# Order of the first three chunks, the planner's charge for a convolution tap, and a sum over channel tiles made by DMA

## The chip, the cores and the metric

The kernel runs on one core of a Trainium2 chip. Its time is what the device takes for one execution, in microseconds; lower is better. The core has TensorE (PE, matmuls), VectorE (DVE, elementwise work with two inputs), ScalarE (ACT, one-input functions), GpSimd (POOL, which here mostly issues DMAs that add to their target) and SyncE (SP, which issues the plain DMAs). Every engine works through its own instructions in order and waits on semaphores for the others.

## What is computed

One layer of a decoder trunk on x of 1024 positions by 1024 channels, float32:

```python
h = rms_norm(x, g_mix)
z = h @ w_in + b_in
va, ga, xb, gb, sa, sb = split(z)            # 1024, 1024, 1536, 1536, 1024, 1024
u = va * sigmoid(ga)
u = causal_depthwise_conv(u, conv_a_w, conv_a_b)       # 31 taps
y_a = silu(layer_norm(u, ln_g, ln_b)) @ w_a_out
v = rg_lru(causal_depthwise_conv(xb, conv_b_w, conv_b_b), ...)   # 4 taps, 16 heads, a scan
y_b = (v * gelu(gb)) @ w_b_out
x = x + (sigmoid(sa) * y_a + sigmoid(sb) * y_b) @ w_o
f = square(relu(rms_norm(x, g_mlp) @ w_1))
out = rms_norm(x + f @ w_2, g_final)
```

The layer norm needs, at each position, the mean over the 1024 channels of the convolved u.

## The kernel before

**Numbers.** Matmuls run on float32 values that are split in a high part h (the rounded value) and a low part l (the rest); a product takes three matmuls, h with h, h with l and l with h ("hh", "hl", "lh": the weight's part stands first in first_z, so "lh" is the weight's low part and "hl" the input's). The high part is an ACT copy. The low part is a DVE subtraction, or, in split_dma (L63), an ACT copy with its sign turned and a DMA from POOL's queue that adds the value to it in SBUF. Channels lie on the 128 partitions, positions along the free dimension, in two halves hf 0 and 1 of 512.

**The first three chunks** (L117 to L398) are the products of h with three blocks of 128 columns of w_in (block 16 of the xb part, 0 of va, 8 of ga). x comes transposed as xc in eight tiles (two halves, four pairs of channel blocks c) and plain as x in eight tiles for the sums of squares. For half 0 the norm's factor isn't known yet: x_plain and x_plain_low make the parts of x times g_mix, and the products are scaled afterwards by first_scale (L403). For half 1 x_square (L182, ACT), x_root (L195, a Newton root on DVE that leaves four diagonal tiles rd) and x_spread (L208, eight PE matmuls that spread rd over partitions as rb) make the factor first, and x_scaled (L215, DVE then ACT) and x_low (L230) the parts. All vectors of weights lie in one tile vec of 448 columns, of which columns 0 to 7 are g_mix. decay (L265) is a generator of 51 tiny DVE instructions on the recurrence's constants; decay_on(n) issues the next n. idle_mm issues matmuls of ones on nothing, ahead of the first real one. The order of ACT, DVE and PE in this block is written out by hand.

**The chunks after** (s from 3, loop at L797): each slot makes 48 matmuls for a chunk of w_in (chunk_mm, L709), those of a head of the recurrence's gates (head_mm, head_gate), and hands the chunk before to xb_out or u_out. Slot 3 does half 1 first, then scales half 0 of the first three chunks (first_scale) and makes half 0's scaled parts (first_parts, L411: xc scaled eight times, the low part three behind), then does half 0. Later come the z stage (loop at L1013: gates by a Strassen product, weights' parts zo by split_dma four steps ahead), the b branch (L1599 on: eight output tiles j, b_mm), and the branch a, w_o and the MLP.

**The convolution** of tile j is the generator conv(j) (L594): two ACT instructions that start its two accumulators, then 48 DVE steps, mostly taps of a scalar_tensor_tensor over 512 columns (L629), a store of the result to DRAM (yd[j], SP) and a last step that adds it to ysum (L641, L643). Its steps have no place of their own.

**The planner** places them. clk holds a planned time for PE, ACT and DVE; at() adds a cost. later() notes DVE work with a ready time, vector_work(end) issues it in order of ready time, and fill(until) (L433) puts taps into the DVE time that is left over:

```python
    def fill(until):
        while clk["V"] + 0.67 <= until:
...
        def step(cost=0.67):
            at("V", cost)
```

When 4 steps of a convolution are left, the ACT start of the next is issued. In the loops the limit is the planned end of PE's work in the slot. What is left after the z stage is issued in tile j = 0 of the b branch, and all that remains in j = 1 (vector_work(math.inf)).

**The mean.** n_load (L1101) reads the eight yd tiles back in 16 DMAs on SP, emitted in tile j = 0; n_mean (L1112) makes the mean by two products of ysum with a matrix of 1/1024, ahead of tile 2's matmuls; n_center, n_var, n_root and n_scale follow in tiles 2 to 5.

The tile framework puts in the waits: an instruction waits for what it reads, and a new tile waits until its slot was released.

Of the kernel before, what the change touches and what calls it, by code (L numbers as in the profile page):

```python
# [9 lines left out]
F32 = mybir.dt.float32  # L10
# [5 lines left out]
P = 128  # L16
# [14 lines left out]
def trunk_kernel(ctx: ExitStack, tc: tile.TileContext, x, xt_in, xt_eo, vecs, w_in, w_a_out, w_b_out,  # L31
# [92 lines left out]


    vec = cp.tile([P, 448], F32, name="vec")
    nc.gpsimd.dma_start(vec, vecs)
    gmix_c = vec[:, 0:8]
    bin_c = vec[:, 8:64]
# [33 lines left out]
    load_w0(1)  # L163
    load_w0(2)
    for t in range(4, 8):
        load_x(t)
# [164 lines left out]
    with tc.manual_schedule(engines={mybir.EngineType.Activation, mybir.EngineType.DVE,  # L331
# [10 lines left out]

        idle_mm(15)
        rb["tile"] = PS("rb", "ps2")
# [10 lines left out]
        for k in range(8):  # L355
            first_z(1, 0, k, "hh")
            first_z(1, 0, k, "hl")
        decay_on(6)
        first_w(2, "h")
        first_w(2, "l")  # L360
        decay_on(20)
        for t in range(4, 8):
# [6 lines left out]
        x_root(1)  # L369
        decay_on(10)  # L370
        for k in range(8):
            first_z(2, 0, k, "lh")
            if k == 4:
                x_spread(1)

        for c in range(9):
            if c < 8:
                x_scaled(1, c)
            else:
                x_root(0)  # L380
                x_spread(0)
            if 4 <= c < 8:
                x_square(c - 4, nc.scalar)
            if c:
                for which in ("hh", "lh"):
                    first_z(0, 1, c - 1, which)
                x_low(1, c - 1)
                first_z(0, 1, c - 1, "hl")
                for i in range(1, N0):
                    first_z(i, 1, c - 1, "hh")  # L390
                    first_z(i, 1, c - 1, "hl")
        for i in range(1, N0):
            for k in range(8):
                first_z(i, 1, k, "lh")
        decay()
        nc.vector.tensor_scalar(cab2, cab_c, 2.0, None, ALU.mult)
        pairs = caw[:, 8:].rearrange("p (i o j) -> p i o j", o=2, j=8)
        nc.vector.tensor_tensor(csum, pairs[:, :, 0, :], pairs[:, :, 1, :], ALU.add)  # L398


    xu = dp.tile([2, 4, P, S], F32, name="xu")

    def first_scale():  # L403

        rs = rb["d"][:, HALVES[1]]
        nc.scalar.activation(rs, rb[0], AF.Copy)
        for i in range(N0):
            o = z0[i][:, HALVES[0]]
            nc.vector.tensor_tensor(o, o, rs, ALU.mult)

    def first_parts():  # L411
        for c in range(11):
            if c < 8:
                x_scaled(0, c)
            if c > 2:
                x_low(0, c - 3)

# [6 lines left out]
    clk = {"P": 0.0, "A": 0.0, "V": 0.0}  # L424
    MM = 0.227

    def at(e, cost, ready=0.0):
# [5 lines left out]
    def fill(until):  # L433
        while clk["V"] + 0.67 <= until:
            if taps["now"] is None:
# [154 lines left out]


    NE = WA // 2 + 1

    def conv(j):  # L594
# [20 lines left out]

        def step(cost=0.67):
            at("V", cost)
            return True
# [19 lines left out]
        yield step()  # L638
        if j == 0:
            ysum.append(T("ysum"))  # L640
            nc.vector.tensor_copy(ysum[0], acc)  # L641
        else:
            nc.vector.tensor_tensor(ysum[0], ysum[0], acc, add)  # L643
        yield step(1.22)

# [62 lines left out]

    def chunk_mm(s, n0, n1, halves=(0, 1)):  # L709

        wh, wl = wst[s]
        if s not in zps:
            zps[s] = PS(f"z{s}")
        pairs = [x for k in range(8) for x in ((wh, k, 0), (wh, k, 1))] + [(wl, k, 0) for k in range(8)]
        for n in range(n0, n1):
            w, k, part = pairs[n]
            for hf in halves:
                nc.tensor.matmul(zps[s][:, HALVES[hf]], w[:, k, :], xw[k][part][hf],  # L718
                                 start=n == 0, stop=n == 23)
        at("P", len(halves) * (n1 - n0) * MM)  # L720

# [74 lines left out]
    with tc.manual_schedule(engines=ENGINES):  # L796
        for s in range(3, NC1):  # L797
            w_load(s + 2)
            taps["hold"] = s > NC1 - 4
            begun = clk["P"]  # L800
            clk["A"], clk["V"] = max(clk["A"], begun + 0.5), max(clk["V"], begun - 2)

            if s == 3:

                chunk_mm(s, 0, 24, (1,))
                first_scale()
                xb_out(0, zps[0])
                first_parts()
                chunk_mm(s, 0, 24, (0,))
            else:  # L810
# [158 lines left out]
    with tc.manual_schedule(engines=ENGINES):  # L969
# [43 lines left out]
        for n in range(len(zseq) + 2):  # L1013
            for f, *a in ZL.get(n, ()):
                f(*a)
            if n >= L:
                for f, *a in ZX.get(n, ()):
                    f(*a)
            taps["hold"] = n < 2
            clk["A"], clk["V"] = max(clk["A"], clk["P"] + 0.5), max(clk["V"], clk["P"] - 2)  # L1020
            z_get(n - 1, z_post)
# [53 lines left out]
    def b_mm(j):  # L1075
# [5 lines left out]
        else:  # L1081

            todo = [x for w, wl, h, l in ops for x in ((w, h), (w, l), (wl, h))]
        for n, (a, b) in enumerate(todo):
            for hf in range(2):
                nc.tensor.matmul(ps[hf], a, b[:, HALVES[hf]], start=n == 0, stop=n == len(todo) - 1)  # L1086
# [511 lines left out]
    with tc.manual_schedule(engines=ENGINES):  # L1598
        for j in range(8):  # L1599
            clk["A"], clk["V"] = max(clk["A"], clk["P"] + 0.5), max(clk["V"], clk["P"] - 2)  # L1600
            if j == 0:
                b_load(1)
                b_gate(0)
                n_load()
            if j == 2:
                n_mean()
            if j == 4:
# [10 lines left out]
            vector_work(clk["V"])  # L1618
            if j < 2:
                vector_work(math.inf if j else clk["P"] - 0.3)  # L1620
            elif j < 4:
                n_center(j - 2)
# [414 lines left out]
```

## Time and profile before

| what | us |
|---|---|
| median of 3 runs (1558.83 to 1559.73) | 1559.06 |
| the profiled execution, its own time | 1559.14 |
| its span on the core | 1557.3 |
| PE busy in it | 1540.5 |
| DVE busy | 1223.7 |
| ACT busy | 894.8 |
| POOL busy | 184.3 |

The span runs from the first to the last instruction. In rows of the timeline the first number is the start in us from the span's start, the second the length; then engine, line, operation, output <- inputs, partitions x elements, count, and in brackets the engine's idle time before it and who ended it. A row with a count over 1 stands for that many in sequence. The end of a matmul is modelled: rows of 0.39 overlap, and the distance of starts is what a matmul takes of PE. TensorE's granted clock was full in all slices of the span.

### The profile page before, as it was taken

Reading aid. Unit: us, or ns where it says so; the run is one execution under the profiler, and the core shown is the slowest. Engines: PE = TensorE matmul, PEld = TensorE weight load, DVE = VectorE, ACT = ScalarE, POOL = GpSimd, SP = SyncE. Lnnn points to the kernel's source line nnn. Section 1 sums busy time; section 2 is a strip of 40 time slices with the busy share of each in tenths; the row PEclk is TensorE's granted clock in tenths of the full one; section 3 lists DMA queues with packets and bytes.
Section 4 is the critical chain, followed back from the end, with each engine's and each line's share of the span. In section 5 each row is a group of like instructions: output and inputs, shape, how many; then the busy total and the mean of one; then the engine's idle time right before and its main releaser. Section 6 shows DMA issues by size and latency. Waiting matters only on the chain.

```text
span 1557.3 us, 19211 instructions
## 1 busy us (share of the span) xinstructions
PE 1540.5 (99%) x6810; PEld 1264.4 (81%) x6810; DVE 1223.7 (79%) x1648; ACT 894.8 (57%) x1256; POOL 184.3 (12%) x219
## 2 busy tenths in 40 slices
PE   9999999999999999999999999999999999999997
PEld 7788778788888888888888887888888888888886
DVE  6899999979999997467579768866555558888898
ACT  6747575667567667444275767545444475555552
POOL 0000000002222222000022322000000001111110
PEclk9999999999999999999999999999999999999999
DMA  8677968899898779953579978523333779889852
GB/s 343 175 178 175 247 168 220 210 270 242 236 252 209 194 190 235 310 185 97 174 209 300 201 159 218 211 80 109 115 115 111 244 216 230 222 227 224 203 122 109
DMA packets 128944, 308.87 MB, mean 198 GB/s; under 512 B 12960, under 2 KB 30880, under 8 KB 128848
## 3 DMA queue, kind: packets, MB, share of 16 engines
q1 hardware_dynamic: 98400, 231.64, 44.9%
q0 software_dynamic: 30304, 75.74, 26.6%
q8 instruction: 53, 0.87, 0.2%
q14 instruction: 43, 0.35, 0.1%
q10 hardware_dynamic: 144, 0.26, 0.0%
HBM read 148.73 MB, written 58.72 MB: 133 GB/s over the span
## 4 chain that ended last, share of the span: by engine, by line
PE 90%; ACT 4%; DVE 3%; DMA 2%; issue 1%; POOL 0%; DVEq 0%; ACTq 0%; POOLq 0%
PE d L1811 15%; PE z L718 13%; PE yb L1086 8%; PE e L1926 2%; PE keep L1811 2%; PE z L254 1%; PE rg L526 1%; PE rg L528 1%; PE rg L527 1%; DMA w_raw<-in_w_dram 1%; DVE v L478 1%; ACT a L550 0%; DVE xc L217 0%; ACT g L558 0%; DMA vec<-in_vecs_dram 0%
## 5 line engine op out<-in xcount | busy, mean ns | idle before, releaser
L718 PE MATMUL z<-xl,win_h 128*128 128x512 f32 x400 | 125.2, 391 | 1.1 <-DVE xl L232 1.1
L718 PE MATMUL z<-xh,win_h 128*128 128x512 f32 x400 | 124.9, 390 | 0.2 <-ACT win_h L67 0.2
L1823 DVE TENSOR_TENSOR acc<-acc,d 128x1024 f32<-128x1024 f32 x72 | 87.8, 1220 | 33.4 <-PE d L1811 32.8
L718 PE MATMUL z<-xh,win_l 128*128 128x512 f32 x400 | 98.2, 391 | 0.0
L718 PEld LDWEIGHTS z<-xl,win_h 128*128 128x128 f32 x400 | 75.1, 188 | 18.8 <-DVE xl L232 3.2
L718 PEld LDWEIGHTS z<-xh,win_l 128*128 128x128 f32 x400 | 75.1, 188 | 16.8
L718 PEld LDWEIGHTS z<-xh,win_h 128*128 128x128 f32 x400 | 75.0, 188 | 16.6 <-ACT win_h L67 0.6
L629 DVE SCALAR_TENSOR_TENSOR y<-u,vec,y 128x511 f32<-128x511 f32 (+14 forms) x120 | 88.4, 736 | 0.0
L534 ACT ACTIVATE g<-rg,vec 96x1024 f32<-96x1024 f32 x32 | 35.6, 1111 | 85.2 <-PE rg L528 40.0
L629 DVE SCALAR_TENSOR_TENSOR yt<-u,vec,yt 128x511 f32<-128x511 f32 (+6 forms) x112 | 82.6, 737 | 0.0
L629 DVE SCALAR_TENSOR_TENSOR y<-yt,csum,y 128x511 f32<-128x511 f32 (+6 forms) x112 | 82.5, 737 | 0.0
L1492 ACT ACTIVATE o<-s 128x512 fp32r<-128x512 f32 x58 | 34.7, 623 | 52.8 <-DVE s L1477 31.3
L66 POOL DMA_DIRECT2D win_l<-win_raw x25 | 21.8, 871 | 332.4 <-ACT win_l L65 307.0
L478 DVE SCALAR_TENSOR_TENSOR v<-xb,vec,v 128x1023 f32<-128x1023 f32 (+2 forms) x36 | 46.2, 1283 | 8.1 <-ACT v L469 7.2
L1086 PE MATMUL yb<-hgh,wb_h 128*128 128x512 f32 x168 | 52.6, 394 | 0.0
L66 POOL DMA_DIRECT2D zo<-zw x42 | 36.6, 871 | 129.8 <-ACT zo L65 112.9
L1086 PE MATMUL yb<-hgl,wb_h 128*128 128x512 f32 x168 | 51.8, 389 | 0.0
L66 POOL DMA_DIRECT2D db_1l<-wr x7 | 6.1, 870 | 309.4 <-DMA wr<-in_w_dram 254.0
L1086 PE MATMUL yb<-hgh,wb_l 128*128 128x512 f32 x168 | 41.0, 389 | 0.0
L1052 DVE TENSOR_TENSOR o<-s,o 128x512 fp32r<-128x512 f32 x58 | 38.8, 683 | 0.0
L65 ACT ACTIVATE zo<-zw 128x512 fp32r<-128x512 f32 x42 | 26.3, 625 | 20.7 <-PE z2f L903 2.1
L1086 PEld LDWEIGHTS yb<-hgh,wb_h 128*128 128x128 f32 x168 | 31.5, 188 | 7.4 <-issue 1.0
(1778 smaller groups left out, 4667.4 us busy)
## 6 DMA issues: line engine op xcount, KB each, us to landing
w_raw<-in_w_dram SPq DMA_DIRECT2D x36, 512.0 KB, 5.4
fr<-fd SPq DMA_DIRECT2D x32, 512.0 KB, 6.1
wr<-in_w_dram SPq DMA_DIRECT2D x32, 512.0 KB, 6.7
zw<-in_w_in_dram SPq DMA_DIRECT2D x28, 512.0 KB, 5.3
win_raw<-in_w_in_dram SPq DMA_DIRECT2D x25, 512.0 KB, 6.7
win_l<-win_raw POOLq DMA_DIRECT2D x25, 512.0 KB, 6.1
zo<-zw POOLq DMA_DIRECT2D x42, 256.0 KB, 5.5
gates<-zg SPq DMA_DIRECT2D x32, 256.0 KB, 3.8
```

Of the source, the lines that this page charges most:

```text
L65: nc.scalar.activation(l, src, AF.Copy, scale=-1.0)
L66: nc.gpsimd.dma_start(l, src, accum_op=ALU.add)
L478: nc.vector.scalar_tensor_tensor(v[:, d:S], a[:, 0:S - d], cbw_c[:, w * 12 + t:w * 12 + t + 1], v[:, d:S], ALU.mult, ALU.add)
L534: nc.scalar.activation(a, gps.pop((n, gi))[:HD, :], AF.Sigmoid, bias=(ba_c, bx_c)[gi][:, n:n + 1])
L629: nc.vector.scalar_tensor_tensor(o[:, k:], a[:, 0:HS - k], c, o[:, k:], ALU.mult, add)
L718: nc.tensor.matmul(zps[s][:, HALVES[hf]], w[:, k, :], xw[k][part][hf], start=n == 0, stop=n == 23)
L1052: tt(l, src, h.bitcast(F32), ALU.subtract)
L1086: nc.tensor.matmul(ps[hf], a, b[:, HALVES[hf]], start=n == 0, stop=n == len(todo) - 1)
L1492: nc.scalar.activation(o[:, 0], src, AF.Copy)
L1811: nc.tensor.matmul(o, a, b, start=n == 0 and (p != 1 or g == 0), stop=n == len(todo) - 1, skip_group_check=p == 1 and g > 0)
L1823: tt(acc[p, q2], acc[p, q2], ps, ALU.add)
L1926: nc.tensor.matmul(o, a, b, start=n == 0, stop=n == len(todo) - 1)
```

## The change

- Columns 0 to 7 of vec get a small tile gmix of their own, loaded first on SP. vec itself moves from POOL's queue to SP's, behind the third weight.
- 12 idle matmuls in place of 15. Of decay, 14 steps stand ahead of the first root (26 before), 6 behind it, 8 behind the second root; the rest come in slot 5, as before.
- x_spread(1) stands ahead of the third chunk's eight lh matmuls (behind five of them before). Behind the loop over c, x_low(1, 7) stands ahead of x_root(0), and x_spread(0) behind the products of c = 7 (ahead of them before). cab2 and csum move into the loop.
- In slot 3, first_scale(0) alone stands ahead of xb_out; the two others stand between the x_scaled; the eight x_low come after all x_scaled; chunk_mm for half 0 takes the matmuls with the input's low part last in place of those with the weight's.
- A tap is charged TAP = 0.735 in place of 0.67.
- The step that adds to ysum is gone. conv notes (planned DVE time + 9, j); sum_up(now), called at the start of every slot, z step and of tiles 0 and 1 of the b branch, issues from POOL a DMA of yd[j] into ysum, the first a copy, the others adding.
- n_load moves from tile 0 to the end of tile 1, behind the drain of the taps; n_mean moves into tile 2, behind 32 of its 72 matmuls.

```diff
--- before.py
+++ after.py
@@ -123,9 +123,9 @@
         return qp.tile([HD, S], dt, tag=tag, name=name, bufs=4 if tag == "p" else 2)
 
 
+    gmix_c = cp.tile([P, 8], F32, name="gmix")
+    nc.sync.dma_start(gmix_c, vecs[:, 0:8])
     vec = cp.tile([P, 448], F32, name="vec")
-    nc.gpsimd.dma_start(vec, vecs)
-    gmix_c = vec[:, 0:8]
     bin_c = vec[:, 8:64]
     gmlp_c = vec[:, 64:72]
     cab_c = vec[:, 72:80]
@@ -162,6 +162,7 @@
         load_xc(0, c2)
     load_w0(1)
     load_w0(2)
+    nc.sync.dma_start(vec, vecs)
     for t in range(4, 8):
         load_x(t)
     for c2 in range(4):
@@ -340,7 +341,7 @@
             for _ in range(n):
                 nc.tensor.matmul(spare[:, 0:P], ones, ones, start=True, stop=True)
 
-        idle_mm(15)
+        idle_mm(12)
         rb["tile"] = PS("rb", "ps2")
         first_w(0, "h")
         first_w(0, "l")
@@ -355,10 +356,9 @@
         for k in range(8):
             first_z(1, 0, k, "hh")
             first_z(1, 0, k, "hl")
-        decay_on(6)
         first_w(2, "h")
         first_w(2, "l")
-        decay_on(20)
+        decay_on(14)
         for t in range(4, 8):
             x_square(t, nc.scalar)
         for k in range(8):
@@ -367,53 +367,48 @@
             first_z(2, 0, k, "hh")
             first_z(2, 0, k, "hl")
         x_root(1)
-        decay_on(10)
+        decay_on(6)
+        x_spread(1)
         for k in range(8):
             first_z(2, 0, k, "lh")
-            if k == 4:
-                x_spread(1)
 
         for c in range(9):
             if c < 8:
                 x_scaled(1, c)
             else:
+                x_low(1, 7)
                 x_root(0)
-                x_spread(0)
+                decay_on(8)
+            if c == 5:
+                nc.vector.tensor_scalar(cab2, cab_c, 2.0, None, ALU.mult)
+                pairs = caw[:, 8:].rearrange("p (i o j) -> p i o j", o=2, j=8)
+                nc.vector.tensor_tensor(csum, pairs[:, :, 0, :], pairs[:, :, 1, :], ALU.add)
             if 4 <= c < 8:
                 x_square(c - 4, nc.scalar)
             if c:
                 for which in ("hh", "lh"):
                     first_z(0, 1, c - 1, which)
-                x_low(1, c - 1)
+                if c < 8:
+                    x_low(1, c - 1)
                 first_z(0, 1, c - 1, "hl")
                 for i in range(1, N0):
                     first_z(i, 1, c - 1, "hh")
                     first_z(i, 1, c - 1, "hl")
+        x_spread(0)
         for i in range(1, N0):
             for k in range(8):
                 first_z(i, 1, k, "lh")
-        decay()
-        nc.vector.tensor_scalar(cab2, cab_c, 2.0, None, ALU.mult)
-        pairs = caw[:, 8:].rearrange("p (i o j) -> p i o j", o=2, j=8)
-        nc.vector.tensor_tensor(csum, pairs[:, :, 0, :], pairs[:, :, 1, :], ALU.add)
 
 
     xu = dp.tile([2, 4, P, S], F32, name="xu")
 
-    def first_scale():
+    def first_scale(i):
 
         rs = rb["d"][:, HALVES[1]]
-        nc.scalar.activation(rs, rb[0], AF.Copy)
-        for i in range(N0):
-            o = z0[i][:, HALVES[0]]
-            nc.vector.tensor_tensor(o, o, rs, ALU.mult)
-
-    def first_parts():
-        for c in range(11):
-            if c < 8:
-                x_scaled(0, c)
-            if c > 2:
-                x_low(0, c - 3)
+        if i == 0:
+            nc.scalar.activation(rs, rb[0], AF.Copy)
+        o = z0[i][:, HALVES[0]]
+        nc.vector.tensor_tensor(o, o, rs, ALU.mult)
 
 
     VA, GA, XB, GB, SA, SB = 0, 8, 16, 28, 40, 48
@@ -423,6 +418,7 @@
 
     clk = {"P": 0.0, "A": 0.0, "V": 0.0}
     MM = 0.227
+    TAP = 0.735
 
     def at(e, cost, ready=0.0):
         clk[e] = max(clk[e], ready) + cost
@@ -431,7 +427,7 @@
     taps = {"wait": [], "now": None, "next": None, "left": 0, "hold": False}
 
     def fill(until):
-        while clk["V"] + 0.67 <= until:
+        while clk["V"] + TAP <= until:
             if taps["now"] is None:
                 if taps["next"] is None:
                     if not taps["wait"] or taps["hold"]:
@@ -589,6 +585,18 @@
 
 
 
+    summed = []
+
+    def sum_up(now):
+
+        while summed and summed[0][0] <= now:
+            j = summed.pop(0)[1]
+            if not ysum:
+                ysum.append(T("ysum"))
+                nc.gpsimd.dma_start(ysum[0], yd[j])
+            else:
+                nc.gpsimd.dma_start(ysum[0], yd[j], accum_op=ALU.add)
+
     NE = WA // 2 + 1
 
     def conv(j):
@@ -613,7 +621,7 @@
         begun = at("A", 1.24)
         yield True
 
-        def step(cost=0.67):
+        def step(cost=TAP):
             at("V", cost)
             return True
 
@@ -636,12 +644,7 @@
         nc.vector.tensor_tensor(p0[:, 1:], p0[:, 1:], p1[:, 0:HS - 1], add)
         nc.sync.dma_start(yd[j], acc)
         yield step()
-        if j == 0:
-            ysum.append(T("ysum"))
-            nc.vector.tensor_copy(ysum[0], acc)
-        else:
-            nc.vector.tensor_tensor(ysum[0], ysum[0], acc, add)
-        yield step(1.22)
+        summed.append((clk["V"] + 9, j))
 
 
 
@@ -706,12 +709,14 @@
             wst[s] = split_w(wraw.pop(s), [P, 8, P], f"win{s}")
             at("A", 2.1)
 
-    def chunk_mm(s, n0, n1, halves=(0, 1)):
+    def chunk_mm(s, n0, n1, halves=(0, 1), low_last=False):
 
         wh, wl = wst[s]
         if s not in zps:
             zps[s] = PS(f"z{s}")
-        pairs = [x for k in range(8) for x in ((wh, k, 0), (wh, k, 1))] + [(wl, k, 0) for k in range(8)]
+        late, soon = ((wh, 1), (wl, 0)) if low_last else ((wl, 0), (wh, 1))
+        pairs = [x for k in range(8) for x in ((wh, k, 0), (soon[0], k, soon[1]))]
+        pairs += [(late[0], k, late[1]) for k in range(8)]
         for n in range(n0, n1):
             w, k, part = pairs[n]
             for hf in halves:
@@ -798,15 +803,21 @@
             w_load(s + 2)
             taps["hold"] = s > NC1 - 4
             begun = clk["P"]
+            sum_up(begun)
             clk["A"], clk["V"] = max(clk["A"], begun + 0.5), max(clk["V"], begun - 2)
 
             if s == 3:
 
                 chunk_mm(s, 0, 24, (1,))
-                first_scale()
+                first_scale(0)
                 xb_out(0, zps[0])
-                first_parts()
-                chunk_mm(s, 0, 24, (0,))
+                for c in range(8):
+                    x_scaled(0, c)
+                    if c in (2, 4):
+                        first_scale(c // 2)
+                for c in range(8):
+                    x_low(0, c)
+                chunk_mm(s, 0, 24, (0,), True)
             else:
                 chunk_mm(s, 0, 18)
             before, new, nxt = (head_at.get(s + d) for d in (-1, 0, 1))
@@ -1017,6 +1028,7 @@
                 for f, *a in ZX.get(n, ()):
                     f(*a)
             taps["hold"] = n < 2
+            sum_up(clk["P"])
             clk["A"], clk["V"] = max(clk["A"], clk["P"] + 0.5), max(clk["V"], clk["P"] - 2)
             z_get(n - 1, z_post)
             z_get(n - 2, z_post2)
@@ -1082,6 +1094,8 @@
 
             todo = [x for w, wl, h, l in ops for x in ((w, h), (w, l), (wl, h))]
         for n, (a, b) in enumerate(todo):
+            if j == 2 and n == 16:
+                n_mean()
             for hf in range(2):
                 nc.tensor.matmul(ps[hf], a, b[:, HALVES[hf]], start=n == 0, stop=n == len(todo) - 1)
         at("P", 72 * MM)
@@ -1601,9 +1615,6 @@
             if j == 0:
                 b_load(1)
                 b_gate(0)
-                n_load()
-            if j == 2:
-                n_mean()
             if j == 4:
                 n_var(0)
                 n_var(1)
@@ -1617,7 +1628,11 @@
                 b_load(j + 2)
             vector_work(clk["V"])
             if j < 2:
+                sum_up(clk["P"])
                 vector_work(math.inf if j else clk["P"] - 0.3)
+                if j:
+                    n_load()
+                    sum_up(math.inf)
             elif j < 4:
                 n_center(j - 2)
             elif j == 4:
```

## The prediction

> **What bounds the kernel now.** I read the page first: span, busy times, rates.
>
> ```profile
> span 1557.3 us, 19211 instructions
> ...
> PE 1540.5 (99%) x6810; PEld 1264.4 (81%) x6810; DVE 1223.7 (79%) x1648; ACT 894.8 (57%) x1256; POOL 184.3 (12%) x219
> ...
> GB/s 343 175 178 175 247 168 220 210 270 242 236 252 209 194 190 235 310 185 97 174 209 300 201 159 218 211 80 109 115 115 111 244 216 230 222 227 224 203 122 109
> ```
>
> TensorE is busy for all but 16.8 us. The change takes away no matmul that counts, so it can only gain time in which PE stands. The view of waits, for PE alone, names these (total, times, longest):
>
> ```profile
> PE rg L526 <- ACT g L534: 2.0, 3, 0.7
> ...
> PE z L718 <- DVE xl L232: 1.1, 2, 0.5
> PE z L254 <- ACT xh L218: 0.8, 1, 0.8
> ```
>
> Two of the three lie in the first 60 us, where the order is changed. That view hides short ones, so I count against a dense stream: one row of the chain of waits, in the stage of the down projection, gives the spacing of matmuls 128x512, 32.64/144 = 0.2267 us.
>
> ```profile
> 1243.88 32.64 PE d L1811 x144
> ```
>
> **Part 1: the start.** Timeline of four engines, start and duration first:
>
> ```profile
> 1.19 1.89 SPq L150 DMA_DIRECT2D xc<-in_xt_dram  x4
> 1.60 6.41 PE L341 MATMUL spare<-ones 128*128 128x128 f32 x30 [1.60 <-POOL ones L112]
> 4.18 1.06 ACT L248 ACTIVATE w_h<-w_raw 128x1024 fp32r<-128x1024 f32 x1 [1.95 <-DMA w_raw<-in_w_in_dram]
> 5.27 1.23 DVE L250 TENSOR_TENSOR w_l<-w_raw,w_h 128x1024 fp32r<-128x1024 f32 x1 [4.40 <-ACT w_h L248]
> 7.61 5.02 ACT L223 ACTIVATE xh<-xc,vec 128x512 fp32r<-128x512 f32 x8 [2.38 <-DMA vec<-in_vecs_dram]
> 8.37 5.39 DVE L227 SCALAR_TENSOR_TENSOR xl<-xc,vec,xh 128x512 fp32r<-128x512 f32 x8 [1.87 <-ACT xh L223]
> 9.17 0.50 PE L254 MATMUL z<-xl,w_h 128*128 128x512 f32 x1
> 25.35 0.94 PE L254 MATMUL z<-xh,w_l 128*128 128x512 f32 x3
> 27.09 0.51 PE L254 MATMUL z<-xh,w_h 128*128 128x512 f32 x1 [0.80 <-ACT xh L218]
> ```
>
> ACT waited 2.38 us for the whole of vec. With the eight columns of g_mix loaded first on SP, what binds is w_raw, w_h, w_l: VectorE is free at 5.27 + 1.23 = 6.50 but began xl at 8.37, 1.87 later. Every load behind g_mix is issued one issue later, 1.89/4 = 0.47. Gain 1.87 - 0.47 = **1.4**. No row shows a transfer of 32-byte rows; its ends are 0 and two issues (0.94), and I take one, the nearest row. The vec load itself goes from POOL's queue to SP's, behind the third weight and ahead of eight x and four xc loads: one more issue for those, the same bytes. Its first reader is then the decay step, not the first chunk. The input must be there too: xc(0) stands right behind w_raw, which ACT had at 4.18, and 512 KB at the first slice's 343 GB/s is 1.5 us, so 5.7 + 0.47 = 6.2, and xh(0) would end by 6.9, just where xl(0) may begin (8.37 - 1.40 = 6.97). Later pairs come 1.5 us apart against 5.39/8 x 2 = 1.35 of xl, so up to 0.5 of the gain can go. The idle matmuls end at 1.60 + 12 x 6.41/15 = 6.7, before the first xh. That cut is worth nothing by itself: 15 of them would end at 8.0 and eat up to 1.2.
>
> From 9.17 PE runs dense until the third chunk's half is done, then stands 0.80 for the first xh of the other half. That comes from the root of the sums of squares:
>
> ```profile
> 18.75 0.19 ACT L191 ACTIVATION_READ_ACCUMULATOR x<-x 128x1 f32 x1
> 20.62 0.16 DVE L198 TENSOR_SCALAR stx<-stx 128x4 f32<-128x4 f32 x1
> 22.12 0.70 ACT L206 ACTIVATE rd<-ident,stx 128x128 f32<-128x128 f32 x2 [1.10 <-DVE stx L105]
> 25.63 1.41 DVE L217 SCALAR_TENSOR_TENSOR xc<-xc,vec,rb 128x512 f32<-128x512 f32 x2 [1.20 <-PE rb L213]
> ```
>
> The squares were there at 18.94, the root began at 20.62, held by decay steps ahead of it on VectorE (14 now, 26 before). It takes 20.62 to 22.82, 2.2. Afterwards it may run 19.4 to 21.6, one issue late included. PE, 1.4 earlier and without the 0.80, starts the other half at 27.09 - 2.2 = 24.9; x_spread(1), at most 1.16 (the other spread's row, below), and eight matmuls (1.81) stand ahead of that, so PE asks at 21.9, 0.3 after the root's end. From rb to the first matmul is 25.63 to 27.09 = 1.46, under the 1.81 that now cover it. Gain **0.8**; if x rows land 0.4 later still, the rest is lost one for one.
>
> **Part 2: the fourth chunk.**
>
> ```profile
> 39.15 1.16 PE L213 MATMUL rb<-rd,ones 128*128 128x128 f32 x8 [0.39 <-DVE rd L204]
> 40.35 0.60 ACT L406 ACTIVATE rd<-rb 128x512 f32<-128x512 f32 x1 [0.84 <-PE rb L213]
> 43.88 1.24 ACT L469 ACTIVATE v<-xb,vec 128x1024 f32<-128x1024 f32 x1
> 46.22 2.71 DVE L217 SCALAR_TENSOR_TENSOR xc<-xc,vec,rb 128x512 f32<-128x512 f32 x4
> 50.85 0.39 PE L718 MATMUL z<-xh,win_h 128*128 128x512 f32 x1
> 53.89 2.50 DVE L232 TENSOR_TENSOR xl<-xc,xh 128x512 fp32r<-128x512 f32 x4
> 54.01 0.63 ACT L218 ACTIVATE xh<-xc 128x512 fp32r<-128x512 f32 x1 [0.63 <-DVE xc L217]
> 57.91 1.05 ACT L67 ACTIVATE win_h<-win_raw 128x1024 fp32r<-128x1024 f32 x1
> 59.01 0.73 PE L718 MATMUL z<-xh,win_h 128*128 128x512 f32 x2 [0.21 <-ACT win_h L67]
> ```
>
> The second half of chunk 3 (24 matmuls, 5.44) took 50.85 to 59.01 = 8.16: PE went at the pace of xh and xl in turn. In the clock of before: x_spread(0) moves behind seven matmuls (1.59), which covers the 0.39 it waited, so rb is 1.20 later but PE is 0.39 earlier. ACT's v ends at 43.88 + 1.24 + 1.20 = 46.3; eight xh at VectorE's 2.71/4 = 0.68 end at 51.7. PE begins the half at 50.46 and asks for an xh every two matmuls, the last at 53.6: covered. VectorE does one scale and, from 42.2, ten more (eight xc, two scales) at 0.68: 49.7 with the first; then eight xl at 2.50/4 = 0.63: 54.7. PE, with the low inputs last, asks for the last xl at 55.7: covered. PE ends at 55.9. But ACT goes on from its last xh to win_h of the next chunk, 54.64 to 59.01 = 4.37, table load and sigmoid included: 51.7 + 4.4 = 56.1, which then sets chunk 4. Gain 59.0 - 56.1 = **2.9**. It is the step that waits next; if ACT loses cover there, each us costs one.
>
> csum and cab2, 0.4 us on VectorE, move into the loop over c, where ACT's squares already set the pace: nothing.
>
> **Part 3: TAP and the sum.** Two taps in order, the last add to ysum, and two stretches (PE busy, PEld, DVE, ACT, POOL):
>
> ```profile
> 136.26 0.74 DVE L629 SCALAR_TENSOR_TENSOR y<-yt,csum,y 128x507 f32<-128x507 f32 x1
> 136.92 0.74 DVE L629 SCALAR_TENSOR_TENSOR yt<-u,vec,yt 128x507 f32<-128x507 f32 x1
> 607.22 1.22 DVE L643 TENSOR_TENSOR ysum<-ysum,y 128x1024 f32<-128x1024 f32 x1
> 608.40:638.10 29.70, 29.70 (x132) 24.59 (x131) 16.59 (x18) 24.25 (x35) 4.66 (x6) 1.00 1.05 316
> 638.10:654.70 16.60, 16.60 (x75) 13.75 (x74) 7.39 (x8) 4.38 (x6) 0.00 (x0) 1.00 0.74 254
> ```
>
> A tap lasts 0.74, but taps follow each other every 0.66: **the old 0.67 was the right charge, 0.735 is the duration**. So the plan now asks less of VectorE than it can do. Per convolution 48 steps x 0.065 - 1.22 for the sum = +1.9 of planned time, 15.2 for eight. The last one ended at 608.4; behind it VectorE has 29.70 - 16.59 = 13.1 free until 638.1 and 16.60 - 7.39 = 9.2 in the first output tile of the b branch: it fits, and ends near 645. PE did not wait for taps before, so nothing is gained. The adds that leave VectorE, 1.22 the last, were hidden too.
>
> The three PE waits for g (2.0) hang on ACT, not on taps, as VectorE stood ready before v:
>
> ```profile
> 145.06 3.92 DVE L478 SCALAR_TENSOR_TENSOR v<-xb,vec,v 128x1023 f32<-128x1023 f32 x3 [0.85 <-ACT v L469]
> 262.32 0.80 ACT L611 ACTIVATE y<-u,vec 128x512 f32<-128x512 f32 x1
> ```
>
> They stay. But the two ACT instructions that open convolution 3 (0.80 each) stood at 262.3, ahead of that chain; two to three convolutions at +1.9, with VectorE half theirs there, move them 8 to 11 us, into it. Ends 0 and **1.6**; I take 0.6, as either side of the exp steps is about as likely and some of it can be hidden.
>
> n_mean moves 32 matmuls into the third output tile: the same four matmuls. n_load moves behind the drain of the taps and so behind b_load(3) and two stores on SP; the loads of weights and gates that stood behind it come earlier. n_center is due after the mean, which is later by 7.3, and the variance two tiles on: nothing.
>
> The eight adds become eight POOL issues. Each waits for a store of 512 KB, nine planned us after its last tap, and what stands behind it on POOL are the low parts zo. Landing times of zo, the page's issue of an accumulate of 512 KB, and the tightest zo with the PE group that reads it (its third matmul):
>
> ```profile
> DMA to landing us min/median/max: 3.2/5.8/8.9
> win_l<-win_raw POOLq DMA_DIRECT2D x25, 512.0 KB, 6.1
> 503.73 0.87 POOL L66 DMA_DIRECT2D zo<-zs  x1 [3.67 <-ACT zo L65]
> 511.40 0.62 PE L903 MATMUL z6e<-xh,zo 128*128 128x512 f32 x2
> ```
>
> The lead is 7.67, the median landing 5.8. Ends: 0, and 5.8 + 6.1 - 7.67 = 4.2 for each of the five sums that fall into this stage. I take 0: 256 KB and 512 KB land nearly alike (5.8, 6.1), so the length of a transfer ahead is a small part of a landing.
>
> **Sum** against the profiled execution: 1559.14 - 1.4 - 0.8 - 2.9 + 0.6 = **1554.6** (span 1552.8); that execution lies 0.08 above the median of the runs.
>
> **Rivals.**
> - *The inputs set the start.* If loads land as late as 1.5 us apart and later, part 1 gives little, and part 2, which hangs on ACT, stays: 1559.1 - 2.9 + 0.6 = 1556.8. For it: the queue is busy from the start; against it: ACT's eight xh ran 5.02 without a pause.
> - *The head waits go too.* If the new placing of taps opens the ACT chain: 1554.6 - 0.6 - 2.0 = 1552.0. Against it: the idle 0.85 above.
> - *zo behind the sums* (slower). One queue, one order: a zo that must let the whole accumulate pass lands late, and PE stands in the z stage. At half the end above, 2.1 x 5 = 10.5: 1565.1. It decides from 1.9 us of delay at the tightest lead. The Trainium skill, "DMA: Bandwidth & Descriptors", section "Queues, rings and completion order", has each DMA engine go round the queues packet by packet, and its section "Two DMAs through the same engine are not ordered" has descriptors of one queue start in order: that speaks for this rival. By the same page's fit of bytes over 436 GB/s (section "Anatomy of one DMA") 512 KB are an estimate of 1.2 us, and the sum would stay 1554.6. No run here shows an accumulate in front of a zo.
> - *The plan spills over* (slower; the change does not do what it says, since 0.735 is no spacing). If a whole convolution (48 x 0.66 = 31.7) is left at 654.7, its store and sum (6.1 each) end at 698.6; PE asks at 638.1 + 176 x 0.2267 = 678.0: 20.6 of waiting, 1575. It decides from 11 us left.
>
> **How the numbers follow.** Forecast 0.55, inputs 0.18, head waits 0.12, zo 0.10, spill 0.05. A measurement here tells 0.2%, 3.1 us. Faster: 0.55 + 0.12 = 0.67; within: 0.18; slower: 0.15. Range: from 1551 (forecast with 1.87 in place of 1.4, no 0.6, head waits gone) to 1560, which holds the inputs' case with the ACT term at its end of 1.6 (1557.8) and 2 us of late zo (the tightest lead allows 1.9), and leaves out the two slower ones.
>
> **What would show it.** First matmul with xl near 7.8, the other half from 24.9, chunk 4 at 53.9, PE dense between; the waits for L232 and L218 gone, those for g kept; the last tap after 630; no PE wait on zo or ysum. The forecast is wrong if PE gets a new wait after 60 us, or if chunk 4 starts later than 56.

## The result, and the profile after

The changed kernel takes 1563.20 us (median of 10 runs, 1561.14 to 1567.62) against 1559.39 for the kernel before in the same series: ratio 1.0026, 95% interval 1.0018 to 1.0035. It is slower by 0.26%; the forecast was 1554.6. Its profiled execution took 1564.42, span 1562.6.

The head of its page:

```profile
span 1562.6 us, 19201 instructions
...
PE 1541.3 (99%) x6804; PEld 1265.6 (81%) x6804; DVE 1215.6 (78%) x1640; ACT 895.4 (57%) x1256; POOL 188.7 (12%) x226
```

The start came as forecast. PE's timeline (start, length), first matmul with xl, the other half, chunk 4:

```profile
8.08 0.50 PE L255 MATMUL z<-xl,w_h 128*128 128x512 f32 x1
...
25.16 0.40 PE L255 MATMUL z<-xh,w_h 128*128 128x512 f32 x1
...
53.53 0.61 PE L723 MATMUL z<-xh,win_h 128*128 128x512 f32 x2
```

Before, these stood at 9.17, 27.09 and 59.01: chunk 4 starts 5.5 us earlier. The span is 5.3 longer, so PE must lose some 11 us behind that. PE's waits name the places (total, times, longest):

```profile
PE z L723 <- ACT win_h L67: 5.2, 1, 5.2
PE rg L522 <- ACT g L530: 2.0, 3, 0.7
PE rg L524 <- DMA vl<-vtl: 1.9, 1, 1.9
...
PE mu L1129 <- DMA ysum<-yd: 0.6, 1, 0.6
```

The second line was there before. The first (win_h, the high part of a chunk's weight), the third (vl, the low part of a head's v) and the fourth (the sum for the mean) are new. PE's timeline around two of them:

```profile
305.57 0.45 PE L524 MATMUL rg<-vl,rgh 96*96 96x512 f32 x1 [1.89 <-DMA vl<-vtl]
...
306.55 1.02 PE L723 MATMUL z<-xh,win_h 128*128 128x512 f32 x2
...
352.37 3.79 PE L723 MATMUL z<-xh,win_l 128*128 128x512 f32 x16
361.37 1.22 PE L723 MATMUL z<-xh,win_h 128*128 128x512 f32 x2 [5.21 <-ACT win_h L67]
```

And two stretches of it (PE, PEld, DVE, ACT, POOL busy, then the granted clock):

```profile
306.50:309.70 3.20, 3.20 (x9) 2.48 (x9) 3.20 (x6) 0.00 (x0) 0.00 (x0) 0.51 1.01 239
...
361.50:364.40 2.90, 2.90 (x7) 2.32 (x8) 2.76 (x5) 1.70 (x2) 0.63 (x2) 0.50 0.87 167
```

Behind each of the two longer waits PE works at half its clock for about 3 us: 0.43 a matmul in place of 0.227. Counted from start to start (the distance of two starts, less the 0.227 that a matmul takes), the wait for vl cost 2.1 and its slow matmuls 1.7, the wait for win_h 5.4 and 1.6, the mean 0.8. That is 11.6, of which a wait near 970 us, 1.3 shorter than before, gives a little back. The view of waits doesn't show what follows a wait; the distance of starts does.

Why win_h came late, from VectorE's and ScalarE's timelines of the changed kernel (the scan's four instructions start at 352.00):

```profile
327.79 1.23 DVE L450 TENSOR_TENSOR xs<-xs,xs 128x1024 f32<-128x1024 f32 x1 [12.98 <-DMA xs<-xu]
...
352.00 1.22 DVE L563 SCALAR_TENSOR_TENSOR g<-a,g 128x1024 f32<-128x1024 f32 x1
...
357.01 1.28 ACT L577 ACT_TABLE_LOAD   x1 [3.83 <-DVE g L566]
...
360.27 1.05 ACT L67 ACTIVATE win_h<-win_raw 128x1024 fp32r<-128x1024 f32 x1
```

VectorE stood 13 us for xs (x's scaled parts, read back from DRAM) and 1.05 more for the next xs, then worked without a pause up to the scan at 352.00: 21 steps of convolution 3 stood between. ACT's sigmoid of u, whose table load is the third row, waited for the scan, and win_h stood behind it. The same place in the kernel before (VectorE, then ACT, then PE):

```profile
347.31 0.68 DVE L636 TENSOR_TENSOR y<-y,yt 128x511 f32<-128x511 f32 x1
348.02 1.22 DVE L643 TENSOR_TENSOR ysum<-ysum,y 128x1024 f32<-128x1024 f32 x1
349.17 1.22 DVE L567 SCALAR_TENSOR_TENSOR g<-a,g 128x1024 f32<-128x1024 f32 x1
...
351.85 1.28 ACT L581 ACT_TABLE_LOAD   x1 [2.08 <-DVE g L569]
...
354.09 3.79 PE L718 MATMUL z<-xh,win_l 128*128 128x512 f32 x16
```

The scan's first instruction stood at 349.17, which is 8.3 us earlier against chunk 4. PE itself lost 3.8 of these at vl; against the chunk that PE is in (its last sixteen matmuls start at 354.09 before, at 352.37 now) the scan is 4.5 late. The sigmoid is later by 2.3 more: before, the product ahead of the scan released it (L569), now the scan itself (L566). The product released it also in runs 1, 5, 7, 10 and 12 below, in all of which win_h is on time; what decides between the two was not tested. That leaves what made the scan late: the longer tap in the plan, the sums by DMA, or the new order itself.

### The profile page after: what moved, and what is told of

Its sections match the earlier page's. It is cut to its first block, busy times and chain, and to the rows that moved or that the text cites. A ratio compares the mean times of both kernels' runs of the same rounds, so it can differ in the third digit from the quotient of the medians.

```text
span 1562.6 us, 19201 instructions
## 1 busy us (share of the span) xinstructions
PE 1541.3 (99%) x6804; PEld 1265.6 (81%) x6804; DVE 1215.6 (78%) x1640; ACT 895.4 (57%) x1256; POOL 188.7 (12%) x226
## 4 chain that ended last, share of the span: by engine, by line
PE 53%; DMA 1%; DVE 1%; ACT 1%; issue 0%; POOL 0%; DVEq 0%; POOLq 0%; ACTq 0%
PE d L1826 15%; PE yb L1100 6%; PE e L1941 2%; PE keep L1826 2%; DMA w_raw<-in_w_dram 1%; DMA ysum<-yd 1%; PE ga0f L1263 0%; PE go1e L1263 0%; PE go0e L1263 0%; PE go2e L1263 0%; PE go3e L1263 0%; PE f15d L1518 0%; PE f15c L1518 0%; PE f15a L1518 0%; PE f14d L1518 0%; PE f14c L1518 0%
```

## The experiments

Each is the median of its runs, with the ratio to the kernel before of its own series (1559.3 to 1559.4) and a 95% interval.

| kernel | us | ratio |
|---|---|---|
| changed kernel | 1563.20 | 1.0026 [1.0018, 1.0035] |
| 1 order alone | 1553.95 | 0.9966 [0.9954, 0.9979] |
| 2 order, sums by DMA, tap 0.67 | 1565.14 | 1.0034 [1.0022, 1.0046] |
| 3 order, tap 0.72, sum on VectorE | 1561.49 | 1.0008 [0.9999, 1.0017] |
| 4 sums by DMA alone | 1570.93 | 1.0073 [1.0060, 1.0086] |
| 5 as 2, plan as in 1 | 1560.37 | 1.0005 [0.9996, 1.0014] |
| 6 changed, tap 0.64 | 1561.15 | 1.0017 [1.0008, 1.0025] |
| 7 changed, old count to convolution 3 | 1556.20 | 0.9983 [0.9974, 0.9991] |
| 8 changed, old count from convolution 4 | 1565.75 | 1.0041 [1.0029, 1.0053] |
| 9 changed, xs planned when it lands | 1560.21 | 1.0001 [0.9992, 1.0010] |
| 10 as 5, seven sums left out | 1554.84 | 0.9971 [0.9960, 0.9983] |
| 11 as 1, xs planned when it lands | 1554.35 | 0.9967 [0.9954, 0.9979] |
| 12 as 5, sums due after 14 | 1557.62 | 0.9993 [0.9984, 1.0002] |
| 13 changed, seven sums left out | 1559.97 | 1.0003 [0.9994, 1.0013] |
| 14 as 13, xs planned when it lands | 1555.61 | 0.9977 [0.9968, 0.9987] |
| 15 as 5, plain loads for sums | 1554.71 | 0.9968 [0.9956, 0.9981] |

### Which part (1 to 4)

The expectations weigh three theories: A, the higher charge for a tap; B, the sums by DMA; C, the earlier start itself. Run 1 takes the change's first part alone: the hunks of the start and of slot 3, with 0.67 and ysum on VectorE.

> Only the new order of the first three chunks; a tap counted at 0.67 and the sum on VectorE as before. Theory A (the higher count for a tap makes the convolutions slip, and what slips collides at 303, 356 and 681 us): the 5.5 us that the fourth chunk gained come out whole, 1553.9, within 1 us, and PE has no wait for vl near 303, none of 5 us for win_h near 356. Theory B (the sums by DMA make those waits): also 1553.9. Theory C (the earlier start alone shifts the rest against its loads): the waits are here too, and the time is 1559 to 1563.

1553.95: 5.4 us faster, theory C falls. All that PE still waits for there, but for the first instruction of all:

```profile
PE rg L521 <- ACT g L529: 3.2, 3, 1.2
...
PE z L255 <- ACT xh L224: 0.7, 1, 0.7
PE z L255 <- DVE xl L228: 0.2, 1, 0.2
```

Run 2 is the changed kernel with one number put back:

```diff
-    TAP = 0.735
+    TAP = 0.67
```

> The changed kernel with a tap counted at 0.67 again, the sums by DMA and the moved mean kept. Theory A: 1553 to 1555, no wait for vl near 303, none for win_h near 356, the last tap before 620 us. Theory B: the waits of the changed kernel stay, 1561 to 1563. Theory C: 1559 to 1563, as without the sums by DMA.

1565.14, slower still. Theory A falls in this form: the right count does not bring the 5.5 us back. Its waits:

```profile
PE z L722 <- ACT win_h L67: 5.2, 1, 5.2
...
PE z4e L913 <- DMA zo<-zs: 1.4, 1, 1.4
...
PE rg L521 <- DMA vh<-vth: 1.0, 1, 1.0
```

Run 3 has the sum on VectorE again and a tap at 0.72 (the load for the mean and the mean where the changed kernel has them):

```diff
-    TAP = 0.735
+    TAP = 0.72
...
-        summed.append((clk["V"] + 9, j))
+        if j == 0:
+            ysum.append(T("ysum"))
+            nc.vector.tensor_copy(ysum[0], acc)
+        else:
+            nc.vector.tensor_tensor(ysum[0], ysum[0], acc, add)
+        yield step(1.22)
```

> The new order, a tap counted at 0.72 (0.05 of the 0.065), the sum on VectorE as before, the load for the mean and the mean at the changed kernel's places. Theory A: the sum's 1.22 stays in the plan on top, so each convolution is given as much planned time as or more than in the changed kernel (48 x 0.05 = 2.4 more than before, against 1.9): the waits near 303 and 356 come, 1559 to 1563. Theory B: no such waits, 1553 to 1555.

1561.49, and PE waits for win_h without any sum by DMA:

```profile
PE z L716 <- ACT win_h L67: 6.4, 1, 6.4
PE rg L522 <- ACT g L530: 2.0, 3, 0.7
```

So theory B alone falls too: 0.72 costs 7.5 us over run 1 (with the load and the mean moved, which by runs 10 and 15 below costs nothing that can be told), and there is no wait for vl or vh. Run 4 adds only the sums by DMA, with the moved load and mean, to the kernel before.

> The kernel before with the sums by DMA and the moved mean alone; order and 0.67 as before. Theory A: within 1 us of before, 1558.5 to 1560.5. Theory B: 5 to 8 us over before, 1564 to 1567. Theory C: as before.

1570.93, beyond theory B: +11.6, as between runs 1 and 2 (+11.2). Two causes, then, or one that both parts set off. The planner tells. Its arithmetic, carried out without a chip, gives for convolution 3 (slot and planned time of its start, planned time of its end):

```
run 1                0.67 + 1.22    slot 19, 213    slot 25, 288
run 2                0.67           slot 20, 230    318
changed kernel       0.735          slot 20, 230    329
run 3                0.72 + 1.22    slot 20, 230    333
run 6, see below     0.64           slot 19, 213    slot 25, 283
```

A small shift of the plan, by a higher charge or by one that is missing, puts convolution 3 a slot later, where its start stands behind ACT's exp chain, and its end behind the scan's slot. In run 2 the cause is that the charge of 1.22 is gone: in slot 8 a second step of convolution 1 now fits ahead of the taps of v, and that step takes VectorE's planned clock from 63.83 to ACT's 68.69, so the slot has five taps less; the rest rolls over from slot to slot.

### The sums by DMA (5, 10, 12, 15)

Run 5 is run 2 with the charge left in the plan, so that VectorE's order is that of run 1:

```diff
+        yield step(1.22)
         summed.append((clk["V"] + 9, j))
```

> As the run with the new order and the sums by DMA at 0.67, but the plan still charges 1.22 to VectorE at the end of each convolution, though nothing is issued there: VectorE's order is then that of the order alone. Theory A2 (what costs is not the count itself but where the plan puts convolution 3: its starts on ACT behind the exp chain and its last taps after the load of xs, ahead of the scan): no wait for win_h near 350, the half-rate matmuls behind it gone, 1553 to 1556, the rest being one zo wait of up to 1.6. Theory B (the sums by DMA cost by themselves): 1564 to 1566, as with 0.67 without the charge.

1560.37, between the two. The plan's part of run 2 is 4.8 (1565.1 to 1560.4), and win_h is on time; 6.4 over run 1 remain, most of them as waits for transfers:

```profile
PE z0a L914 <- DMA zo<-zw: 2.2, 1, 2.2
...
PE z13e L914 <- ACT zc L963: 1.4, 1, 1.4
...
PE rg L521 <- DMA vh<-vth: 1.0, 1, 1.0
PE z4e L914 <- DMA zo<-zs: 0.7, 1, 0.7
```

The wait for zc, near 632 us, names ACT; it is gone in runs 10 and 15 too, and what leads to it was not followed. Run 10 leaves the adding transfers out of run 5, run 15 makes plain loads of them:

```diff
             else:
-                nc.gpsimd.dma_start(ysum[0], yd[j], accum_op=ALU.add)
...
-                nc.gpsimd.dma_start(ysum[0], yd[j], accum_op=ALU.add)
+                nc.gpsimd.dma_start(ysum[0], yd[j])
```

> The sums by DMA with VectorE's old order (1560.4), with seven of the eight transfers left out: ysum is then convolution 0's result alone. Stores of y, the moved load and the moved mean stay. If the accumulating transfers cost the 6.4 us over the order alone: 1553.5 to 1555.5, no waits for vh near 303, zo near 364 and 471. If the moved load and mean, or chance, cost them: 1559 to 1561.

> The sums by DMA with VectorE's old order (1560.4), the seven accumulating transfers replaced by loads of the same 512 KB into the same tile (ysum is then convolution 7's result alone). If the price lies in the bytes and the places in the queues: 1559 to 1561.5. If it lies in the adding: 1554 to 1557, as without the transfers.

1554.84 and 1554.71: without them, and with loads of the same bytes at the same places, the price is gone. The stores, the moved load, the moved mean and VectorE's missing adds change nothing that can be told (0.9 over run 1, the intervals overlap). It is the adding that costs. The software queue's row of the page, first run 5:

```profile
q0 software_dynamic: 31392, 79.71, 28.0%
```

Run 15, the same packets and bytes:

```profile
q0 software_dynamic: 31392, 79.71, 27.4%
```

Run 10, seven transfers less:

```profile
q0 software_dynamic: 30384, 76.04, 26.9%
```

The shares are of 16 DMA engines' span. By the difference from run 10, seven adding transfers hold 1.1% of it, 17 us, 2.4 each; seven plain ones 0.5%, 1.1 each. As the shares are rounded to a tenth, each of the two is good to about a quarter of a us. Taken packet by packet from the traces, each of the four sums in the z stage held the engines 2.6 to 3.0 us in run 5 and 1.3 to 1.4 in run 15. The sums' rows in the two traces, time from issue to landing, run 5:

```profile
DMA to landing us min/median/max: 6.2/8.6/10.8
```

Run 15:

```profile
DMA to landing us min/median/max: 4.7/6.5/9.0
```

Run 12 moves the due time of each sum from 9 to 14 behind its last tap. In run 5, GpSimd had stood before a store that had not landed:

```profile
356.61 0.87 POOL L597 DMA_DIRECT2D ysum<-yd  x1 [2.64 <-DMA yd<-y]
357.98 0.89 POOL L66 DMA_DIRECT2D zo<-zw  x1 [0.50 <-ACT zo L65]
```

```diff
-        summed.append((clk["V"] + 9, j))
+        summed.append((clk["V"] + 14, j))
```

> The sums by DMA with VectorE's old order (1560.4), each sum planned 14 us behind its last tap in place of 9. If the price is GpSimd standing before a store that has not landed (2.64 near 356, zo behind it): the zo wait of 2.4 near 364 goes, 1557 to 1559. If it is the transfer itself that delays what lands beside or behind it: the waits only move, 1559.5 to 1562.

1557.62, as the first theory had it, though not all of the wait near 364 went: from 2.4 to 1.1 start to start; the other waits for zo are gone, the one for vh stays at 1.2. So some 2.8 of the 6.4 hung on when GpSimd issued the sums; the intervals of the two runs overlap a little, so the size is rough. What the rest hangs on was not taken apart.

### The plan (6 to 9, 11)

Run 6 counts a tap at 0.64, below its true 0.655.

> The changed kernel with a tap counted at 0.64, less than the 0.655 it takes. In this plan convolution 3 starts one chunk earlier than at 0.67 and is over before the last two chunks. Theory A2: no wait for win_h near 350, 1553.5 to 1557, though the count is wrong. Rival A (a right count is what matters; 0.64 makes taps late against the plan, 0.655 to 0.67 would be best): not faster than the 1565 of 0.67. Theory B: 1563 to 1566.

1561.15, a miss of theory A2's range. Convolution 3 was out of the way, but the plan used the room to start convolution 4 in slot 24, ahead of the same scan: PE waited 2.9 start to start for win_h, at half clock for eight matmuls after. With the sums' own price on top, 1554 was never to be had. Rival A falls as well: the wrong count beats 0.67 by 4.0.

Runs 7 and 8 split the count by convolution. In run 7 steps take 0.67 and the charge stays up to convolution 3, and 0.735 comes after; run 8 has it the other way round:

```diff
+        if j < 4:
+            yield step(1.22)
+        if j == 3:
+            TAP[0] = 0.735
         summed.append((clk["V"] + 9, j))
```

> The changed kernel with the old count (0.67 and 1.22 at the end) for convolutions 0 to 3 and 0.735 from convolution 4 on. Theory A2: the waits near 303 and 356 and the half-rate matmuls behind them go, the wait of the mean for the last sum stays (about 1): 1554 to 1556. Theory B: 1561 or more.

> The changed kernel with 0.735 for convolutions 0 to 3 and the old count from convolution 4 on. Theory A2: waits near 303 and 356 as in the changed kernel, no wait of the mean: 1561.5 to 1563. Theory B, if the late last sums are what costs: 1555 to 1557.

1556.20 and 1565.75. The early count makes 7.0 of time (changed kernel less run 7), and no wait for win_h or vl is in run 7. The late count does not cost, it helps: 2.5 between run 8 and the changed kernel (their intervals overlap), 4.2 between runs 5 and 7, where the waits near 471 (0.9) and 632 (1.5) of run 5 are gone; why, was not tested. The mean's wait, expected in run 7, did not come.

Run 9 tests the chain from xs to win_h itself. The subtractions on xs are planned later, so that taps fill the wait:

```diff
-            later(0, 1.2, nc.vector.tensor_tensor, q[n], q[a], q[b], ALU.subtract)
+            later(0 if c2 else clk["P"] - 1, 1.2, nc.vector.tensor_tensor, q[n], q[a], q[b],
+                  ALU.subtract)
```

> The changed kernel, with the four subtractions on the first xs planned one us before the end of their chunk (about when xs lands) and not at its start. The number of taps up to the scan is the same; they now fill the 13 us in which VectorE stood waiting for xs. Theory A2 (the taps of convolution 3 left behind that wait hold up the scan, that the sigmoid of u, that win_h): the wait near 356 (5.4) and the half-rate matmuls behind it (1.8) go, the rest stays: 1555 to 1558. Rival (win_h is held by where ACT's own work stands, not by VectorE): 1562 to 1565.

1560.21. VectorE no longer stands for xs (it now stands 8.2 for u and 3.6 for g):

```profile
332.99 4.99 DVE L450 TENSOR_TENSOR xs<-xs,xs 128x1024 f32<-128x1024 f32 x4
...
348.53 1.22 DVE L563 SCALAR_TENSOR_TENSOR g<-a,g 128x1024 f32<-128x1024 f32 x1
```

The scan is 3.5 earlier. Not all of that is the wait: 19 taps stand in the plan's two slots ahead of the scan where the changed kernel has 21, and two taps are 1.3. PE's waits are:

```profile
PE rg L524 <- DMA vl<-vtl: 2.1, 1, 2.1
...
PE z L724 <- ACT win_h L67: 1.1, 1, 1.1
PE rg L522 <- DMA vh<-vth: 1.1, 1, 1.1
PE z0a L915 <- DMA zo<-zw: 0.9, 1, 0.9
```

The wait for win_h fell from 5.4 to 1.3 start to start, and its slow matmuls are all but gone: the chunk takes 12.5 in place of 17.9, 5.4 back, as theory A2 says, and the rival falls. Only 3.0 came out, because waits for vh (1.2) and zo (1.1) were new and vl 0.3 longer. Run 11 makes the same edit in run 1 (and admits no new convolution from one slot earlier on).

> The new order alone (1553.95) with the first xs subtractions planned late as above, and no new convolution from one chunk earlier on. VectorE stands less, but PE has no wait there to lose: 1553.3 to 1554.6 by every theory; under 1553 would show that a shorter wait than the list names hangs on it.

1554.35, no gain: in run 1 nothing hangs on it.

### Both causes in the changed kernel (13, 14)

Run 13 is the changed kernel without the seven adding transfers (the edit of run 10), run 14 that with the edit of run 9.

> The changed kernel with seven of the eight sums by DMA left out (ysum is convolution 0's result alone); plan and VectorE's order unchanged. Theory C2 (two prices side by side: the accumulating transfers make heads' loads, low parts and the mean late; the plan makes the scan and so win_h late): the wait for vl near 303 (2.1), the half-rate matmuls behind it (1.7) and the mean's wait (0.8) go, that for win_h near 356 (5.4 + 1.8) stays: 1557.5 to 1559.5. Rival (the transfers also make xs late, and through it win_h): both go, 1551 to 1554.

> The changed kernel with both: seven of the eight sums left out and the first xs subtractions planned when xs lands. Theory C2: what the two prices leave is the new order's time, 1552 to 1555, with the count still at 0.735. Rival (the count has a price of its own behind 400 us): 1556 or more.

1559.97 and 1555.61. In run 13 the waits for vl and for the mean are gone and one is left:

```profile
PE z L721 <- ACT win_h L67: 4.1, 1, 4.1
```

So the rival (one cause) falls, though win_h is 1.2 less late: the transfers had a small part in it. How they made vl late shows in the landing of the head's three loads near 300, changed kernel:

```profile
DMA to landing us min/median/max: 6.0/8.3/9.7
```

Run 13:

```profile
DMA to landing us min/median/max: 5.8/7.4/7.7
```

13 brings 3.2, 9 brings 3.0, both together 7.6 of the 9.3 between the changed kernel and the order alone. 1.7 are left, with intervals that overlap; run 14 still waits 1.2 for win_h and 0.9 for zo. Whether the count itself costs anything beyond that stays open. Run 1 has the lowest median and beats both kernels; runs 10, 11 and 15 can't be told from it.

## Why the forecast failed

**Start and fourth chunk** (1.4 + 0.8 + 2.9 = 5.1): right in kind and in sum. Chunk 4 came 5.5 earlier; the terms measured 1.1, 0.8 and 3.6. The third is larger because ACT did not set chunk 4: its win_h began at 50.92 and was over when PE came to it, dense, at 53.53. The order alone is 5.4 faster, but that it is so near to 5.5 is luck: in run 1 the three waits for g, which were to stay, are 1.2 longer, and the wait near 970, 1.7 before, is gone.

**ACT's starts** (+0.6): the end 0 was true. The starts of convolution 3 stood at 274.6, in ACT's chain and 17.8 later against chunk 4, where 8 to 11 were forecast; yet the three stalls before the heads were as before, 0.83 each.

**"It fits, and ends near 645. PE did not wait for taps before, so nothing is gained"**: this step failed. It sized the plan's slip as 1.9 per convolution, and looked at it at two places, the starts of convolution 3 on ACT and the end of the last one. The planner fills slots, so a small change of a charge moves a convolution by a whole slot; convolution 7 ended at 666.6, not 645. And convolution 3 has a limit of its own, which the trace of before showed: its last add was at 347.31 and the scan began at 349.17, with only the add to ysum (1.22) between. That the sign of "nothing" could be a loss was not asked of that row. Price: 7.0 in the changed kernel's trace (5.4 and 1.6). Of the 6.8 by which the sigmoid was late against PE, 2.3 came from what released it, which the forecast did not look at and no run tested alone.

**The sum by DMA, taken as 0 between 0 and 4.2 for each of five**: the size was wrong, the kind was in the text. "256 KB and 512 KB land nearly alike" compared sizes, and both of those rows were adding transfers; the engines' time of one, about twice that of a load, is in neither. The trace of before held it: its adding packets of 4096 bytes took 348 ns each, 2.8 us of the 16 engines for 512 KB. Cost: 6.4 with VectorE's old order, of which 5.5 go when the transfers go.

**zo behind the sums**: real in runs 2, 4, 5, 6, 7, 9 and 12, with waits of 0.7 to 2.2 in the lists, but at one or two places, not five; in the changed kernel none hit zo. There the same transfers hit vl, a load of another queue, which no rival named. Not every wait for zo is the sums' doing: runs 10 and 14, without them, have 0.3 and 0.7.

**The plan spills over**: in small, yes. The rival was to decide from 11 us left at 654.7. 11.9 were left (666.6 less 654.7; some 3 less if that mark goes with PE, which was ready for the mean at 681.2 and not at 678.0), and the mean waited 0.8.

So 1554.6 was 1559.1 less 5.1 plus 0.6. The 5.1 were there, as 5.5; the two zeros in the middle, the plan's slip and the sums, cost 9.3 together (the changed kernel less run 1).

## What to carry to other kernels

Ask of a planner's charge where each piece of work lands, slot by slot, and which later instruction on the same engine stands right behind it; an average slip says little. An engine that is 20% idle can still be the one that is late at one place. Moving an add from a free engine to the DMA engines costs their time, and who pays is whatever lands beside it: replace the transfer by a plain load of the same bytes to see that price alone.

## What the runs showed of the hardware

An adding DMA of 512 KB from DRAM to SBUF held the DMA engines 2.6 to 3.0 us against 1.3 to 1.4 for a plain load (by packets; 2.4 against 1.1 by the rounded shares), and landed in 8.6 against 6.5 (medians, runs 5 and 15).

A wait of TensorE can cost more than its length. Behind 2.1 and 5.4 us of standing (changed kernel) and behind 2.9 (run 6) the granted clock was 0.50 to 0.51 for some 3 us (3.4 in the changed kernel, from 306.5 to 309.9 and from 361.4 to 364.8); behind 2.4 (run 5) it stayed full:

```profile
367.20:370.60 3.40, 3.40 (x15) 2.82 (x16) 1.82 (x2) 1.04 (x3) 0.12 (x1) 1.00 1.07 206
```

So length alone doesn't decide. The Trainium skill, "TensorE: Matmul & The Clock Gate", section "What's actually happening", has the clock set by free-running windows of 3.4 us, of which an idle one halves it. The length of the slow stretches agrees; that a standing of 2.1 us, shorter than a window, sufficed does not fit an idle window, and the measurement decides.

VectorE's taps of 128 x 507 last 0.74 and follow each other every 0.66, after as before; no run asked what the overlap is.
